# Attention over 64 heads: first and last pair head by head, loads in a new order, a fixed plan for the values

## The chip, the cores and the metric

The kernel runs on one core of a Trainium2 chip. The metric is the device time of one execution in microseconds (us). The profiler's span, from the first to the last instruction, is about 1.8 us shorter (134.32 us and 132.5 us for the profiled run of the kernel before). A run is called slow here when it is more than 1.5% above the fastest run of the same kernel; kernels are compared by their fast runs, and a difference under 2% is not called faster or slower. Five engines matter: TensorE (PE in the profile, with its weight loads as PEld), VectorE (DVE), ScalarE (ACT), GpSimd (POOL), and SyncE (SP), which issues most transfers.

## The reference

```python
q, k, v: float32 [8, 8, 512, 64]          # batch, heads, sequence, dim
scores = einsum('bhqd,bhkd->bhqk', q, k) / 8
attn   = exp(scores - max) ; attn = attn / attn.sum(-1)
out    = einsum('bhqk,bhkd->bhqd', attn, v)
```

The kernel leaves out the maximum and divides at the end: v carries a column of ones, so the value matmuls give the row sums as column 65.

## The kernel before

The 64 heads are 32 pairs. Both heads of a pair lie in one 128-row tile, 64 rows each. Scores are made transposed, in blocks of 128 keys x 512 queries. Two blocks form a group: one `st` buffer in PSUM, the memory that TensorE writes to (two banks; a bank is the unit in which the kernel shares it out), one exponential on ScalarE. A pair is four groups, numbered through from 0. The code is abridged:

```python
ps_st = tile_pool(bufs=3)   # scores, 2 banks each: 6 banks
ps_o  = tile_pool(bufs=1)   # o, the values' result: 1 bank
ps_t  = tile_pool(bufs=1)   # transposes: 1 bank
...
def values(g, h, part):                 # one part = four matmuls
    if part == 0:
        os[(g, h)] = ps_o.tile([P, NI, D + 1], FP32, tag="o")   # waits for the last reader
    for x in range(NI):
        nc.tensor.matmul(o[:, qc, :], blocks[...], vps[...])     # qc, c from part and x
    if part == NI - 1:
        normalise(g, h)                 # VectorE: reciprocal, product, o is free after it
...
fill = []                               # work that is put between the scores, in this order
for g in range(NP):
    for h in range(2):
        transposes(g + 2, 1 - h)        # two halves
        values(g, h, 0..3)
...
for m in range(steps):                  # after the scores of group m: up to 6 entries of fill,
    scores(m)                           # as far as their exponentials are LAG groups old
    ...
```

(A quota and the age of the exponentials decide how many entries follow. What comes of it in the steady state is: scores, all four value parts of head 0, four transposes, scores, all four parts of head 1, four transposes, scores, scores.) For the last pair both heads' values are summed key block by key block.

The softmax here doesn't subtract the row's maximum and nothing guards it: scores larger than these inputs give would overflow.

## Time and profile before

| | before |
|---|---|
| device time, median of the first 3 runs | 134.61 us (134.34 to 134.69) |
| span of the profiled run | 132.5 us |
| ScalarE busy | 119.3 us, 90% |
| TensorE busy, as recorded | 102.2 us, 77% |
| one pair (four groups) in the steady state | 3.67 us |
| first exponential | 6.04 us |
| scores of group 126 (of 128) to the end of the span | 132.5 - 122.93 = 9.6 us |

ScalarE is full in the middle, so the pair's 3.67 us is its time for four exponentials. The prediction below shows the lines.

Two kinds of lines are shown. A group line gives line of the kernel, engine, operation, output<-input, sizes and count, then busy us and mean ns of one, then the engine's idle time before them and what ended it. A timeline line starts with start and length in us; a bracket at its end gives the idle time before it and what ended that. `vp` is v, `pt` the exponentials, `tqk` the transposed q and k, `tp` a transpose's result, `ob` the divided output.

### The profile page before, as it was taken

How to read it: one execution, taken by the hardware profiler on the slowest of the kernel's cores; microseconds unless marked ns; L12 is line 12 of the kernel's file. 1: busy time of each engine (PE TensorE's matmuls, PEld its weight loads, DVE VectorE, ACT ScalarE, POOL GpSimd, SP SyncE). 2: the span in 40 equal slices, each digit the busy share in tenths (PEclk: the TensorE clock that was granted, in tenths of full speed). 3: DMA queues.
4: the chain of work that ended last, by engine and by line, in shares of the span. 5: the costliest groups of instructions: out<-in, count | busy, mean ns of one | idle time of the engine just before them, and what ended most of it. 6: DMA issues, size and time to landing. Idle time of an engine off the chain costs nothing.

```text
span 132.5 us, 3980 instructions
## 1 busy us (share of the span) xinstructions
PE 102.2 (77%) x1542; PEld 63.7 (48%) x1542; DVE 61.3 (46%) x196; ACT 119.3 (90%) x130; POOL 56.7 (43%) x107
## 2 busy tenths in 40 slices
PE   6737988777877778877788777898777877778650
PEld 2222755554555455555455544555544554454440
DVE  0412464455445555445544455544454445554231
ACT  3264999999999999999999999999999999999910
POOL 2268887544445555534444555534544445000000
PEclk9965799999999999999999999999999999999975
DMA  3999999989998999969999889949999990222231
GB/s 112 274 354 354 348 355 335 340 297 267 299 303 209 324 314 318 294 181 311 333 302 307 285 284 291 307 143 304 350 337 283 293 297 28 75 77 79 79 117 47
DMA packets 35123, 33.82 MB, mean 255 GB/s; under 512 B 2080, under 2 KB 35104, under 8 KB 35104
## 3 DMA queue, kind: packets, MB, share of 16 engines
q1 hardware_dynamic: 34832, 33.43, 79.0%
q8 instruction: 12, 0.20, 0.6%
q10 hardware_dynamic: 272, 0.13, 0.3%
q14 instruction: 7, 0.06, 0.2%
HBM read 25.17 MB, written 8.39 MB: 253 GB/s over the span
## 4 chain that ended last, share of the span: by engine, by line
ACT 41%; PE 33%; issue 13%; DVE 4%; DMA 4%; SPq 1%; POOL 0%; ACTq 0%
ACT pt L125 41%; PE o L157 16%; PE st L117 11%; PE tp L104 6%; DMA k<-in_k_dram 4%; DVE ob L136 3%; DVE rc L135 1%; DVE tqk L106 1%; POOL qkp L90 0%; SPq L176 0%; SPq L175 0%; SPq L174 0%; ACTq L125 0%
## 5 line engine op out<-in xcount | busy, mean ns | idle before, releaser
L125 ACT ACTIVATE pt<-st 128x1024 f16<-128x1024 f32 x128 | 117.7, 1351 | 4.7 <-PE st L117 4.7
L117 PE MATMUL st<-tqk 64*128 64x512 f16 x256 | 45.0, 389 | 14.2 <-ACT pt L125 14.0
L157 PE MATMUL o<-vp,pt 128*128 128x65 f16 x1024 | 44.6, 196 | 8.1 <-DVE ob L136 8.1
L157 PEld LDWEIGHTS <-pt 128*128 128x128 f16 x1024 | 36.6, 99 | 24.7 <-DVE ob L136 16.5
L90 POOL CAST qkp<-k 128x512 f16<-128x512 f32 x31 | 19.0, 613 | 46.9 <-PE tp L104 44.3
L135 DVE RECIPROCAL rc<-o 128x4 f32<-128x4 f32 x64 | 11.7, 183 | 57.3 <-PE o L157 57.3
L117 PEld LDWEIGHTS <-tqk 64*128 64x128 f16 x256 | 14.3, 94 | 32.7 <-issue 24.5
L136 DVE TENSOR_TENSOR ob<-o,rc 128x256 f32<-128x256 f32 x64 | 27.2, 425 | 2.5 <-DVE rc L135 0.3
L106 DVE COPY tqk<-tp 128x512 f16<-128x512 f16 x62 | 25.7, 415 | 4.6 <-PE tp L104 4.6
L104 PE MATMUL tp<-ident,qkp 128*128 128x128 f16 x248 | 24.7, 224 | 2.9 <-POOL qkp L90 1.9
L83 POOL CAST vp<-v 128x512 f16<-128x512 f32 x32 | 19.7, 616 | 3.6 <-DMA v<-in_v_dram 2.7
L90 POOL CAST qkp<-q 128x512 f16<-128x512 f32 x31 | 19.0, 613 | 0.6 <-DMA q<-in_q_dram 0.2
L104 PEld LDWEIGHTS <-qkp 128*128 128x128 f16 x248 | 15.4, 99 | 3.9 <-POOL qkp L90 3.6
L232 PE MATMUL warm<-zeros 128*128 128x512 f16 x6 | 2.7, 629 | 1.2 <-DVE zeros L226 1.2
L186 ACT ACT_TABLE_LOAD x1 | 1.3, 1283 | 1.2 <-PEq L272 1.2
L232 PEld LDWEIGHTS <-zeros 128*128 128x128 f16 x6 | 0.7, 136 | 2.3 <-DVE zeros L226 1.2
L184 DVE CAST qkp<-k 128x256 f16<-128x256 f32 x1 | 0.3, 294 | 2.9 <-DMA k<-in_k_dram 2.9
L187 POOL CAST qkp<-k 128x256 f16<-128x256 f32 x1 | 0.4, 396 | 2.9 <-DMA k<-in_k_dram 2.9
L186 ACT CAST qkp<-q 128x256 f16<-128x256 f32 x1 | 0.4, 405 | 1.3 <-DMA q<-in_q_dram 1.3
L193 PEld LDWEIGHTS <-qkp 128*128 128x128 f16 x2 | 0.1, 106 | 1.4 <-DVE qkp L184 1.4
L193 PE MATMUL tp<-ident,qkp 128*128 128x128 f16 x2 | 0.3, 229 | 0.5 <-DVE qkp L184 0.5
L226 DVE MEMSET zeros<- 128x256 uint32 x1 | 0.3, 272 | 0.9 <-PEq L272 0.9
(15 smaller groups left out, 3.6 us busy)
## 6 DMA issues: line engine op xcount, KB each, us to landing
q<-in_q_dram SPq DMA_DIRECT2D x32, 256.0 KB, 4.3
v<-in_v_dram SPq DMA_DIRECT2D x32, 256.0 KB, 4.6
k<-in_k_dram SPq DMA_DIRECT2D x31, 256.0 KB, 4.2
out_dram<-ob SPq DMA_DIRECT2D x31, 256.0 KB, 3.2
out_dram<-ob SPq DMA_DIRECT2D x2, 128.0 KB, 2.2
k<-in_k_dram ACTq DMA_DIRECT2D x1, 128.0 KB, 3.3
k<-in_k_dram SPq DMA_DIRECT2D x1, 128.0 KB, 3.1
```

The costliest lines, as they stand in the source:

```text
L83: nc.gpsimd.tensor_copy(out=vps[g % NV][:, :, :, 0:D], in_=raw[g]["v"][:, :, :, :])
L90: nc.gpsimd.tensor_copy(out=t[:, n].rearrange("p i (h d) -> p h i d", h=2), in_=raw[g][name][:, :, :, :],)
L104: nc.tensor.transpose(tp[:, i, :], qkp[g][:, n, i, :], ident)
L106: nc.vector.tensor_copy(out=tqk[g][:, n, :], in_=tp.rearrange("p i c -> p (i c)"))
L117: nc.tensor.matmul(st[:, x, :], tqk[g][po : po + 64, 1, c * P : (c + 1) * P], tqk[g][po : po + 64, 0, :], start=True, stop=True,)
L125: nc.scalar.activation(out=pt[:, 0:size, :], in_=st[:, 0:size, :], func=EXP, scale=scale)
L135: nc.vector.reciprocal(out=rc[:, :, :], in_=o[:, :, D : D + 1])
L136: nc.vector.tensor_tensor(out=ob[:, h], in0=o[:, :, 0:D], in1=rc[:, :, :].broadcast_to([P, NI, D]), op=AluOp.mult,)
L157: nc.tensor.matmul(o[:, qc, :], blocks[NB * g + 2 * c + h][:, qc * P : (qc + 1) * P], vps[g % NV][:, h, c, :], start=(c == 0 and (qc == 0 ...
L186: nc.scalar.copy(q16[:, 1], tiles["q"][:, 1])
L187: nc.gpsimd.tensor_copy(out=k16[:, :, 2:4], in_=tiles["k"][:, :, 2:4])
L232: nc.tensor.matmul(warm[:, 0, :], zeros[:, 0:P], zeros[:, :], start=True, stop=True)
```

## The change

The intent is to shorten both ends. The first pair's q and k are loaded as halves, one head each, and its scores are taken head by head. Each later pair's q and k are loaded before the v of the pair before it. The last pair is taken head by head too, with the last group split into two of one block, so that little is left after the last exponential. The quota rule is replaced by a fixed list.

```diff
-    NB = 2 * NI
-    TOTAL = NP * NB
+    stream = []
+    for g in range(NP):
+        if g in (0, LAST):
+            stream += [(g, c, h) for h in range(2) for c in range(NI)]
+        else:
+            stream += [(g, c, h) for c in range(NI) for h in range(2)]
+    groups = [stream[n : n + 2] for n in range(0, len(stream), 2)]
+    tail = groups.pop()
+    groups += [[b] for b in tail]
 ...
     def values(g, h, part):
+        last = g == LAST and h == 1
         if part == 0:
-            os[(g, h)] = ps_o.tile([P, NI, D + 1], FP32, tag="o", name=f"o_{g}_{h}")
+            pool, tag = (ps_t, "tp") if last else (ps_o, "o")
+            os[(g, h)] = pool.tile([P, NI, D + 1], FP32, tag=tag, name=f"o_{g}_{h}")
 ...
+    def first_loads():
+        for h in range(2):
+            nc.scalar.dma_start(out=tk[:, h], in_=source(k, 0)[:, h])
+            nc.sync.dma_start(out=tq[:, h], in_=source(q, 0)[:, h])
 ...
-    for g in range(NP):
-        for h in range(2):
-            if g + 2 < NP:
-                for part in range(2):
-                    fill.append((-1, transposes, (g + 2, 1 - h, part)))
-            for part in range(NI):
-                need = ...
-                fill.append((need, values, (g, h, part)))
+    for g in range(NP - 1):
+        if g == 0:
+            fill[2] += [(transposes, (1, 1)), (transposes, (1, 0))]
+        else:
+            fill[4 * g + 1].append((transposes, (g + 1, 1)))
+            fill[4 * g + 2].append((transposes, (g + 1, 0)))
+        todo = [(values, (g, h, part)) for h in range(2) for part in range(NI)]
+        for m, n in ((6, 2), (7, 3), (8, 2), (9, 1)) if g < LAST - 1 else ((6, 3), (7, 3), (8, 2)):
+            fill[4 * g + m] += todo[:n]
+            todo = todo[n:]
+    fill[M - 1] += [(values, (LAST, h, part)) for h in range(2) for part in range(NI)]
 ...
+        load(1, "kq")
+        load(0, "v")
+        for g in range(2, 6):
+            load(g, "kq")
+            load(g - 1, "v")
```

Cut: the first pair's casts and transposes, now per head, the loop that walks the list, and the transposes, which are now made one pair ahead instead of two.

More of the change, by code (lines that the diff above doesn't have):

```diff
@@ L13 @@
 AluOp = mybir.AluOpType
-GROUP = 2
-ST_BUFS = 3
-LAG = 3
 @with_exitstack
@@ L36 @@
     ppb = H // 2
-    NB = 2 * NI
-    TOTAL = NP * NB
+    LAST = NP - 1
+    stream = []
[7 more added lines that the diff above has]
+    groups += [[b] for b in tail]
+    M = len(groups)
     cpool = ctx.enter_context(tc.tile_pool(name="const", bufs=1))
@@ L43 @@
     tpool = ctx.enter_context(tc.tile_pool(name="tqk", bufs=4))
-    ppool = ctx.enter_context(tc.tile_pool(name="pt", bufs=24 // GROUP))
+    ppool = ctx.enter_context(tc.tile_pool(name="pt", bufs=12))
     opool = ctx.enter_context(tc.tile_pool(name="out", bufs=4))
-    ps_st = ctx.enter_context(
-        tc.tile_pool(name="ps_st", bufs=ST_BUFS, space=bass.MemoryType.PSUM)
-    )
+    ps_st = ctx.enter_context(tc.tile_pool(name="ps_st", bufs=3, space=bass.MemoryType.PSUM))
     ps_o = ctx.enter_context(tc.tile_pool(name="ps_o", bufs=1, space=bass.MemoryType.PSUM))
@@ L63, with load_tile, load, cast_qk @@
     obs = {}
-    def where(g):
-        return g // ppb, 2 * (g % ppb)
     def source(src, g):
-        b, h = where(g)
+        b, h = g // ppb, 2 * (g % ppb)
         return src[b, h : h + 2].rearrange("h (p i) d -> p h i d", i=NI)
-    def load(g):
+    def load_tile(g, name):
+        t = lpool.tile([P, 2, NI, D], FP32, tag=f"{name}32", name=f"{name}32_{g}")
+        raw.setdefault(g, {})[name] = t
+        return t
+    def load(g, names):
         if g >= NP:
             return
-        tiles = {}
-        for name, src in (("k", k), ("q", q), ("v", v)):
-            t = lpool.tile([P, 2, NI, D], FP32, tag=f"{name}32", name=f"{name}32_{g}")
+        for name in names:
+            src = {"q": q, "k": k, "v": v}[name]
+            t = load_tile(g, name)
             nc.sync.dma_start(out=t[:, :, :, :], in_=source(src, g))
-            tiles[name] = t
-        raw[g] = tiles
     def cast_v(g):
         nc.gpsimd.tensor_copy(out=vps[g % NV][:, :, :, 0:D], in_=raw[g]["v"][:, :, :, :])
-    def cast(g):
+    def cast_qk(g):
         if g >= NP:
@@ L94, in cast, with transposes @@
         qkp[g] = t
-        cast_v(g)
-    def transposes(g, n, part):
-        if part == 0:
-            if n == 1:
-                tqk[g] = tpool.tile([P, 2, S], FP16, tag="tqk", name=f"tqk_{g}")
-            tps[g] = ps_t.tile([P, NI, P], FP16, tag="tp", name=f"tp_{g}_{n}")
-        tp = tps[g]
-        for i in (2 * part, 2 * part + 1):
+    def transposes(g, n):
+        if g >= NP:
+            return
+        if n == 1:
+            tqk[g] = tpool.tile([P, 2, S], FP16, tag="tqk", name=f"tqk_{g}")
+        tp = ps_t.tile([P, NI, P], FP16, tag="tp", name=f"tp_{g}_{n}")
+        for i in range(NI):
             nc.tensor.transpose(tp[:, i, :], qkp[g][:, n, i, :], ident)
-        if part == 1:
-            nc.vector.tensor_copy(out=tqk[g][:, n, :], in_=tp.rearrange("p i c -> p (i c)"))
+        nc.vector.tensor_copy(out=tqk[g][:, n, :], in_=tp.rearrange("p i c -> p (i c)"))
     def scores(m):
-        n0 = m * GROUP
-        size = min(GROUP, TOTAL - n0)
-        st = ps_st.tile([P, GROUP, S], FP32, tag="st", name=f"st_{m}")
-        pt = ppool.tile([P, GROUP, S], FP16, tag="pt", name=f"pt_{m}")
-        for x in range(size):
-            g, j = divmod(n0 + x, NB)
-            c, h = divmod(j, 2)
+        grp = groups[m]
+        size = len(grp)
+        st = ps_st.tile([P, 2, S], FP32, tag="st", name=f"st_{m}")
+        pt = ppool.tile([P, 2, S], FP16, tag="pt", name=f"pt_{m}")
+        for x, (g, c, h) in enumerate(grp):
             po = 64 * h
@@ L123, in scores @@
             )
-            blocks[n0 + x] = pt[:, x, :]
+            blocks[(g, c, h)] = pt[:, x, :]
         nc.scalar.activation(
@@ L141, in normalise @@
         )
-        last = g == NP - 1
-        if last:
+        if g == LAST:
             nc.sync.dma_start(out=source(out, g)[:, h], in_=ob[:, h])
@@ L148, in values @@
     def values(g, h, part):
+        last = g == LAST and h == 1
         if part == 0:
-            os[(g, h)] = ps_o.tile([P, NI, D + 1], FP32, tag="o", name=f"o_{g}_{h}")
+            pool, tag = (ps_t, "tp") if last else (ps_o, "o")
+            os[(g, h)] = pool.tile([P, NI, D + 1], FP32, tag=tag, name=f"o_{g}_{h}")
         o = os[(g, h)]
-        last = g == NP - 1
         for x in range(NI):
@@ L158, in values @@
                 o[:, qc, :],
-                blocks[NB * g + 2 * c + h][:, qc * P : (qc + 1) * P],
+                blocks[(g, c, h)][:, qc * P : (qc + 1) * P],
                 vps[g % NV][:, h, c, :],
@@ L166, in values @@
             normalise(g, h)
-    def first_pair():
-        tiles = {}
-        for name in ("k", "q", "v"):
-            tiles[name] = lpool.tile([P, 2, NI, D], FP32, tag=f"{name}32", name=f"{name}32_0")
-        raw[0] = tiles
-        nc.scalar.dma_start(out=tiles["k"][:, :, 0:2], in_=source(k, 0)[:, :, 0:2])
-        nc.sync.dma_start(out=tiles["q"][:, :, :, :], in_=source(q, 0))
-        nc.sync.dma_start(out=tiles["k"][:, :, 2:4], in_=source(k, 0)[:, :, 2:4])
-        nc.sync.dma_start(out=tiles["v"][:, :, :, :], in_=source(v, 0))
@@ L178, in first_transposes @@
-    def first_transposes():
-        tiles = raw[0]
-        t = qpool.tile([P, 2, NI, P], FP16, tag="qkp", name="qkp_0")
-        qkp[0] = t
-        k16 = t[:, 1].rearrange("p i (h d) -> p h i d", h=2)
-        q16 = t[:, 0].rearrange("p i (h d) -> p h i d", h=2)
-        nc.vector.tensor_copy(out=k16[:, :, 0:2], in_=tiles["k"][:, :, 0:2])
-        nc.vector.tensor_copy(out=q16[:, 0], in_=tiles["q"][:, 0])
-        nc.scalar.copy(q16[:, 1], tiles["q"][:, 1])
-        nc.gpsimd.tensor_copy(out=k16[:, :, 2:4], in_=tiles["k"][:, :, 2:4])
-        cast_v(0)
-        tqk[0] = tpool.tile([P, 2, S], FP16, tag="tqk", name="tqk_0")
-        tk = ps_t.tile([P, NI, P], FP16, tag="tp", name="tp_0_1")
-        tq = ps_o.tile([P, NI, P], FP16, tag="o", name="tp_0_0")
-        for i in range(2):
-            nc.tensor.transpose(tk[:, i, :], t[:, 1, i, :], ident)
-        nc.vector.tensor_copy(
-            out=tqk[0][:, 1, 0:256], in_=tk[:, 0:2].rearrange("p i c -> p (i c)")
-        )
-        for i in range(NI):
-            nc.tensor.transpose(tq[:, i, :], t[:, 0, i, :], ident)
-        nc.vector.tensor_copy(out=tqk[0][:, 0, :], in_=tq.rearrange("p i c -> p (i c)"))
-        tk2 = ps_t.tile([P, 2, P], FP16, tag="tp", name="tp_0_2")
-        for i in range(2):
-            nc.tensor.transpose(tk2[:, i, :], t[:, 1, 2 + i, :], ident)
-        nc.vector.tensor_copy(
-            out=tqk[0][:, 1, 256:512], in_=tk2.rearrange("p i c -> p (i c)")
-        )
@@ L208 @@
-    fill = []
-    for n in (1, 0):
-        for part in range(2):
-            fill.append((-1, transposes, (1, n, part)))
-    for g in range(NP):
-        for h in range(2):
-            if g + 2 < NP:
-                for part in range(2):
-                    fill.append((-1, transposes, (g + 2, 1 - h, part)))
-            for part in range(NI):
-                need = NB * g + 2 * (part if g == NP - 1 else NI - 1) + h
-                fill.append((need, values, (g, h, part)))
-    AHEAD = 5
@@ L222 @@
-    with tc.manual_schedule():
-        first_pair()
-        for g in range(1, AHEAD):
-            load(g)
+    def first_loads():
+        tk = load_tile(0, "k")
+        tq = load_tile(0, "q")
+        for h in range(2):
+            nc.scalar.dma_start(out=tk[:, h], in_=source(k, 0)[:, h])
+            nc.sync.dma_start(out=tq[:, h], in_=source(q, 0)[:, h])
+    def first_transposes():
+        tk, tq = raw[0]["k"], raw[0]["q"]
+        tqk[0] = tpool.tile([P, 2, S], FP16, tag="tqk", name="tqk_0")
+        halves = []
+        for h in range(2):
+            t = cpool.tile([P, 2, NI, P], FP16, name=f"qkp_0_{h}")
+            nc.gpsimd.memset(t[:, :, :, 64 * (1 - h) : 64 * (1 - h) + 64], 0.0)
+            halves.append(t)
+        for h in range(2):
+            t, s = halves[h], slice(64 * h, 64 * h + 64)
+            if h == 0:
+                nc.vector.tensor_copy(out=t[:, 1, 0:2, s], in_=tk[:, h, 0:2])
+                nc.vector.tensor_copy(out=t[:, 0, 0:2, s], in_=tq[:, h, 0:2])
+                nc.scalar.copy(t[:, 0, 2:4, s], tq[:, h, 2:4])
+                nc.gpsimd.tensor_copy(out=t[:, 1, 2:4, s], in_=tk[:, h, 2:4])
+            else:
+                nc.gpsimd.tensor_copy(out=t[:, 1, :, s], in_=tk[:, h])
+                nc.gpsimd.tensor_copy(out=t[:, 0, :, s], in_=tq[:, h])
+        for h in range(2):
+            t, s = halves[h], slice(64 * h, 64 * h + 64)
+            pk = ps_t.tile([P, NI, P], FP16, tag="tp", name=f"tp_0_1_{h}")
+            pq = ps_o.tile([P, NI, P], FP16, tag="o", name=f"tp_0_0_{h}")
+            for n, i in ((1, 0), (1, 1), (0, 0), (0, 1), (0, 2), (0, 3), (1, 2), (1, 3)):
+                if (n, i) == (1, 2):
+                    pk2 = ps_st.tile([P, 2, P], FP16, tag="st", name=f"tp_0_2_{h}")
+                dst = pq[:, i, :] if n == 0 else pk[:, i, :] if i < 2 else pk2[:, i - 2, :]
+                nc.tensor.transpose(dst, t[:, n, i, :], ident)
+                if (n, i) == (1, 1):
+                    nc.vector.tensor_copy(
+                        out=tqk[0][s, 1, 0:256], in_=pk[s, 0:2].rearrange("p i c -> p (i c)")
+                    )
+                elif (n, i) == (0, 3):
+                    nc.vector.tensor_copy(
+                        out=tqk[0][s, 0, :], in_=pq[s].rearrange("p i c -> p (i c)")
+                    )
+                elif (n, i) == (1, 3):
+                    nc.vector.tensor_copy(
+                        out=tqk[0][s, 1, 256:512], in_=pk2[s].rearrange("p i c -> p (i c)")
+                    )
+            if h == 0:
+                scores(0)
+                scores(1)
@@ new lines @@
+    fill = [[] for _ in range(M)]
+    for g in range(NP - 1):
+        if g == 0:
+            fill[2] += [(transposes, (1, 1)), (transposes, (1, 0))]
+        else:
+            fill[4 * g + 1].append((transposes, (g + 1, 1)))
[4 more added lines that the diff above has]
+            todo = todo[n:]
@@ L226 @@
+    fill[M - 1] += [(values, (LAST, h, part)) for h in range(2) for part in range(NI)]
+    with tc.manual_schedule():
+        first_loads()
+        load(1, "kq")
[3 more added lines that the diff above has]
+            load(g - 1, "v")
         nc.vector.memset(zeros[:, :], 0.0)
@@ L229 @@
             nc.gpsimd.memset(vps[n][:, :, :, D : D + 1], 1.0)
-        warm = ps_st.tile([P, GROUP, S], FP32, tag="st", name="warm")
+        warm = ps_st.tile([P, 2, S], FP32, tag="st", name="warm")
         for n in range(6):
@@ L233 @@
         first_transposes()
-        cast(1)
-        cast(2)
-        done = 0
-        steps = (TOTAL + GROUP - 1) // GROUP
-        for m in range(steps):
-            n0 = m * GROUP
-            if n0 % NB < GROUP:
-                g = n0 // NB
-                load(g + AHEAD)
-                cast(g + 3)
-            scores(m)
-            quota = max(0.0, (n0 + GROUP) * len(fill) / TOTAL)
-            budget = GROUP * 3
-            while done < len(fill) and done < quota and budget > 0:
-                need, what, args = fill[done]
-                if need >= (m - LAG + 1) * GROUP:
-                    break
-                what(*args)
-                done += 1
-                budget -= 1
-        while done < len(fill):
-            need, what, args = fill[done]
-            what(*args)
-            done += 1
+        cast_qk(1)
+        cast_v(0)
+        cast_qk(2)
+        cast_v(1)
+        for m in range(M):
+            g, x = divmod(m, 4)
+            if x == 0:
+                load(g + 6, "kq")
+                if g + 5 < NP:
+                    load(g + 5, "v")
+                cast_qk(g + 3)
+                if g + 2 < NP:
+                    cast_v(g + 2)
+            if m >= 2:
+                scores(m)
+            for what, args in fill[m]:
+                what(*args)
 _INS = ['q', 'k', 'v']
```

## The prediction

> **What bounds the kernel now.** I read the page's busy row and its slices first, because they say which engine is full and where it is not.
>
> ```profile
> PE 102.2 (77%) x1542; PEld 63.7 (48%) x1542; DVE 61.3 (46%) x196; ACT 119.3 (90%) x130; POOL 56.7 (43%) x107
> ...
> ACT  3264999999999999999999999999999999999910
> ```
>
> ScalarE (ACT) is full in all slices but the first four and the last two. Its groups, and the TensorE (PE) groups that feed it, are these; the next view is ScalarE's own part of the timeline.
>
> ```profile
> L125 ACT ACTIVATE pt<-st 128x1024 f16<-128x1024 f32 x128 | 117.7, 1351 | 4.7 <-PE st L117 4.7
> L117 PE MATMUL st<-tqk 64*128 64x512 f16 x256 | 45.0, 389 | 14.2 <-ACT pt L125 14.0
> ```
>
> ```profile
> 6.04 2.86 ACT L125 ACTIVATE pt<-st 128x1024 f16<-128x1024 f32 x3 [1.81 <-PE st L117]
> 11.75 114.80 ACT L125 ACTIVATE pt<-st 128x1024 f16<-128x1024 f32 x125 [2.85 <-PE st L117]
> ```
>
> One exponential has a latency of 1.351 us but they overlap: 125 in 114.80 us is (114.80 - 1.351)/124 = 0.915 us from start to start, or 3.66 us for a pair of heads (four groups). So the run is: 6.04 us until the first exponential, a hole of 2.85 us after three, 125 without a hole, and 132.5 - 126.55 = 5.95 us after the last. TensorE waits for ScalarE, which is the sign of its slack. How much slack, and of what kind, is in one period of the steady state, from the timeline:
>
> ```profile
> 71.59 0.39 PE L117 MATMUL st<-tqk 64*128 64x512 f16 x2 [0.48 <-ACT pt L125]
> ...
> 71.92 0.56 PEld L157 LDWEIGHTS <-pt 128*128 128x128 f16 x16 [0.23 <-issue]
> ...
> 72.41 0.24 PEld L104 LDWEIGHTS <-qkp 128*128 128x128 f16 x4
> ...
> 72.64 0.18 DVE L135 RECIPROCAL rc<-o 128x4 f32<-128x4 f32 x1 [1.27 <-PE o L157]
> 72.75 0.10 PEld L117 LDWEIGHTS <-tqk 64*128 64x128 f16 x2
> ...
> 72.85 0.42 DVE L136 TENSOR_TENSOR ob<-o,rc 128x256 f32<-128x256 f32 x1
> ...
> 73.33 0.56 PEld L157 LDWEIGHTS <-pt 128*128 128x128 f16 x16 [0.49 <-DVE ob L136]
> ```
>
> I name the pieces S (a pair of score matmuls), V (four value matmuls, one of the four parts of a head) and T (four transposes). From start to start: S followed by V 0.33 us; four V 0.49, so one V 0.12; T followed by S 0.35. The order is S, 4V, T, S, wait, 4V, T, S, S. The wait is the point: there is one buffer for the output o, so the second head's first V may start only when VectorE has divided the first head's o. From the last V's slot (72.41) to the next V (73.33) is 0.92 us: matmul latency 0.2, reciprocal 0.2, product 0.42, handovers 0.1. In the kernel before, T and S (0.68 us) fill nearly all of it. Near the end, where no T is left, it stands bare:
>
> ```profile
> 123.25 0.56 PEld L157 LDWEIGHTS <-pt 128*128 128x128 f16 x16 [0.23 <-issue]
> ...
> 124.67 0.31 PEld L157 LDWEIGHTS <-pt 128*128 128x128 f16 x8 [0.86 <-DVE ob L136]
> 125.03 0.10 PEld L117 LDWEIGHTS <-tqk 64*128 64x128 f16 x2
> ```
>
> 124.67 - 123.25 = 1.42 us, less 0.49 for the four V, is 0.93 us of standing still. The same lines show that two V followed by S take 0.36, where 0.245 would be their share: a step from V to S costs about 0.11 more.
>
> **What the Trainium skill says.** "TensorE: Matmul & The Clock Gate", Part 2, "Step-by-step: what each phase is for": only weight loads are pulled ahead, the matmuls stay in program order. The trace agrees: nothing overtakes the V that waits at 124.67. So whatever follows a waiting V in the program waits with it. "TensorEngine Tiling (Array Packing)", "Key Properties": changing the tiling mode drains TensorE. Scores use 64 rows, values and transposes 128; the 0.11 us at each change from V to S fits this, though nothing isolates the cause. "DMA: Bandwidth & Descriptors", "Anatomy of one DMA", gives a constant cost of about 2.0 us per transfer; here 128 KB to the output land in 2.2 us (median), so the last transfer cannot shrink below that by being small.
>
> **The change, part by part.**
>
> *Head.* The first pair's q and k now arrive as 128 KB per head, so the first head waits for 256 KB instead of 512 KB. The old loads landed at 3.8 (q) and 4.0 to 4.4 (k). I put the first halves at 3.3 to 3.5 (2.2 us of latency after the issue at 0.74, plus sharing). The warm-up matmuls hold TensorE until about 3.8, so the first scores come at about 5.0 and the first exponential at about 5.4, 0.6 earlier. The hole at 8.9 came from the second pair's k, which was issued at 2.24 and landed at 7.61, 5.37 us in the chain of waits. Moved ahead of v it is issued at about 1.74, and should land where v did before (its cast started at 6.23). Its cast (0.61), q's cast (0.61, q landing near 7.5), two T with the copy between them (0.61, 0.42) put the fourth score group at about 9 and the seventh, S6, where the values begin, at about 11. Before, exponential 6 started at 11.75 + 3 x 0.915 = 14.5, its scores somewhat earlier. The head is worth 2 to 3 us.
>
> *Steady state.* The old rule put all of a head's V in one group. The fixed plan spreads them 2, 3, 2, 1, so that a pair is, in TensorE's program order: S, V00, V01, T, S, V02, V03, V10, S, V11, V12, S, V13, T, and again S, V00. V10 stands directly behind V03 and needs o divided: 0.93 us with nothing to fill it, in every pair. V00 of the next pair stands behind V13, T, S: of 0.93 us, T and S fill 0.68. Work it out as a loop, from V02:
>
> V02 V03 0.245, bare wait 0.93, V10 and the step to S 0.235, S 0.33, V11 V12 and the step 0.36, S 0.33, V13 0.12, wait 0.93 (T and S inside it), V00 V01 0.245, T 0.35, S 0.33. Sum 4.4 us.
>
> The same by content: four S 1.3, eight V 1.0, two T 0.7, two extra steps 0.2: 3.2 us of work, below ScalarE's 3.66. With 0.93 bare and 0.25 half-filled, 4.4. So TensorE's order becomes the bound, with ScalarE idle 0.7 us in each pair. Without any cost for the mode steps, S at 0.21, it would still be near 3.85. I take 4.3. It applies from S6 to S126, 30 periods: 129 us, where ScalarE alone would need 30 x 3.66 = 110. The loss is 19 us.
>
> *Tail.* Head-by-head order and one-block groups were to leave only one V after the last exponential, instead of two heads (126.55 to 129.73). But the plan's pieces of pair 30 come late. From S126: S with both blocks on the same rows 0.54, rest of a wait 0.4, three V 0.37, S and step 0.43, V 0.12, bare wait 0.93, two V and step 0.36, S 0.32, two V 0.25, bare wait 0.93, eight V 0.98, then matmul latency, two divisions in a row, about 1.0: 6.6 us. The last transfer to the end of the span takes as before 132.5 - 129.73 = 2.8. Together 9.4. ScalarE is done well before and saves nothing here.
>
> Sum: 11 + 129 + 9.4 = 149.4 us of span. The median time is 134.61 for a span of 132.5, so 2.1 more: about 151.5; I name 151, since prefetched weight loads may trim a little.
>
> **The rivals.**
>
> *ScalarE stays the bound.* Three score buffers let TensorE run up to two groups ahead, and ScalarE was 90% busy. If the waits were absorbed, the time would be 134.6 less 2 to 3 (head) less 1.5 to 2 (tail), about 130.5. For it: the plan looks balanced, and TensorE stood idle at each ACT wait (0.48 us as recorded, more if the ends of matmuls were real). Against it: buffers absorb an uneven spacing, not a period that is too long, and the period contains two dependent chains through VectorE that sum above 3.66 whatever ScalarE does.
>
> *TensorE bound, but milder.* If S costs 0.21 and the mode steps nothing, the loop is 3.85, and the time 151.5 - 30 x 0.45 = 138. The isolated S, V steps of 0.33 in the trace speak against it.
>
> *Transfers become the bound.* Inputs and outputs are 33.4 MB; early slices reach 354 GB/s, so 34 MB need about 95 us. Not near.
>
> *Slower clock.* The clock row falls to 0.57 in the tail of before, where TensorE is idle for long. If gaps of 0.93 us also lowered it in the steady state, T, V and S would stretch and the time could pass 157. The gaps are short beside the working stretches, so I give it little.
>
> **Range and chances.** The period is the uncertain term: 4.05 to 4.5 gives 30 x 0.45 = 13.5 us of width, from about 144 to 157.5; the head adds 1 us either way, and the mild rival pulls the lower end. I take 142 to 157. For a time below 137.3 the period would have to be under 3.83, which needs both waits nearly hidden: 0.09 in all, of it 0.05 for faster than 131.9, for the case that I misread which tile V10 waits for.
>
> **What would show it.** Right: ScalarE idle before score matmuls some 30 times or more, about 20 us in all; values waiting for the division (PE o <- DVE ob), 8.1 us in 32 waits before, rising to about 30 us in some 60 waits of about 0.9 and 0.25 us; a period of 4.3 us; first exponential near 5.4 and no hole over 1.5 us before the fifth. Wrong: a ScalarE row with 9 in every middle slice, a period of 3.66, or the V after V03 starting within 0.3 us.

## The result, and the profile after

The first four executions of the changed kernel took 154.38, 159.99, 155.65 and 157.87 us, median 156.76, against 134.48 (133.95 to 134.69) before. A ratio is the mean time of one kernel's fast runs over that of the other's of the same rounds, so not quite the ratio of the medians; here it is 1.153 (1.143 to 1.164). The two longer executions count as slow and are left out of it. Four more executions gave 154.0 to 155.5 us and 1.152. They were run at other times.

The page of the changed kernel, its busy row, ScalarE's slices and the groups that answer to those shown of before:

```profile
PE 116.9 (77%) x1550; PEld 68.2 (45%) x1550; DVE 64.9 (43%) x199; ACT 122.5 (80%) x131; POOL 58.2 (38%) x111
...
ACT  4589988988888898888888988888898888889810
...
L126 ACT ACTIVATE pt<-st 128x1024 f16<-128x1024 f32 x129 | 120.9, 1024 | 22.2 <-PE st L118 22.2
L158 PE MATMUL o<-vp,pt 128*128 128x65 f16 x1024 | 60.1, 197 | 29.5 <-DVE ob L137 29.5
```

No engine is full any more. ScalarE stands idle 22.2 us waiting for scores. The recorded mean length of an exponential fell from 1351 to 1024 ns, but the instruction isn't faster: four of them in 3.77 us, as below, are still 0.92 us from start to start. (That it no longer queues behind its neighbour is my reading.) Who waits for whom, in the view of waits (total us, times, longest), first before, then after:

```profile
PE o L157 <- DVE ob L136: 8.1, 32, 0.8
```

```profile
PE o L158 <- DVE ob L137: 29.5, 62, 0.8
ACT pt L126 <- PE st L118: 22.2, 32, 2.0
```

Two waits of TensorE per pair instead of one, and one hole of ScalarE per pair. ScalarE's timeline after (start, length, what; the last line is one of some thirty alike):

```profile
5.65 3.02 ACT L126 ACTIVATE pt<-st 128x1024 f16<-128x1024 f32 x3 [2.02 <-PE st L118]
9.41 8.36 ACT L126 ACTIVATE pt<-st 128x1024 f16<-128x1024 f32 x9 [0.74 <-PE st L118]
...
70.92 3.77 ACT L126 ACTIVATE pt<-st 128x1024 f16<-128x1024 f32 x4 [0.64 <-PE st L118]
```

The first hole has shrunk from 2.85 to 0.74 us, which was intended. Then four exponentials and a hole of 0.64 us, again and again. Here is what TensorE and VectorE do in one such period:

```profile
72.47 0.30 PEld L158 LDWEIGHTS <-pt 128*128 128x128 f16 x8 [0.49 <-DVE ob L137]
...
73.44 0.31 PEld L158 LDWEIGHTS <-pt 128*128 128x128 f16 x8 [0.23 <-issue]
...
73.91 0.18 DVE L136 RECIPROCAL rc<-o 128x4 f32<-128x4 f32 x1 [0.26 <-PE o L158]
74.13 0.42 DVE L137 TENSOR_TENSOR ob<-o,rc 128x256 f32<-128x256 f32 x1
...
74.60 0.18 PEld L158 LDWEIGHTS <-pt 128*128 128x128 f16 x4 [0.86 <-DVE ob L137]
...
74.84 0.10 PEld L118 LDWEIGHTS <-tqk 64*128 64x128 f16 x2
...
75.16 0.31 PEld L158 LDWEIGHTS <-pt 128*128 128x128 f16 x8 [0.23 <-issue]
...
76.88 0.31 PEld L158 LDWEIGHTS <-pt 128*128 128x128 f16 x8 [0.48 <-DVE ob L137]
77.12 0.30 PEld L108 LDWEIGHTS <-qkp 128*128 128x128 f16 x4
```

At 72.47 come head 0's first two parts, at 73.44 its last two, at 73.91 the division starts, and only at 74.60 may head 1's first part enter the single o buffer. Nothing stands between in the program, so TensorE does nothing for 0.9 us. The scores behind it (74.84) come late, and ScalarE has its hole. At 76.88 the next pair's first part waits for head 1's division, behind scores and transposes that hide most of it. One period before and after. The numbers are its length, then the busy time of TensorE, its weight loads, VectorE, ScalarE and GpSimd (with counts), the granted TensorE clock as a share of full speed, the share of the DMA engines, and GB/s:

```profile
71.59:75.26 3.67, 3.00 (x48) 1.92 (x48) 1.88 (x6) 3.67 (x5) 1.73 (x3) 1.00 0.94 300
```

```profile
72.47:76.88 4.41, 3.48 (x48) 2.07 (x48) 1.97 (x7) 3.77 (x5) 1.74 (x3) 1.00 0.59 188
```

The same 48 matmuls at the same full clock, 4.41 us instead of 3.67. That splits the difference of the two spans, 152.6 - 132.5 = 20.1 us:

| stretch | before | after | difference |
|---|---|---|---|
| start to scores of group 6 | 12.82 | 10.49 | -2.3 |
| group 6 to group 126, 30 pairs | 110.1 (3.67 each) | 132.1 (4.40 each) | +22.0 |
| group 126 to the end | 9.6 | 10.0 | +0.4 |

In these two profiles the head gained, the tail didn't, and the middle lost 22 us. (How much of the head's gain is the change, and how much the run, comes up in experiment 8.)

### The profile page after: what moved, and what is told of

Read it like the earlier page. It is cut to its first block, busy times and chain, and to the rows that moved or that the text cites. A ratio compares the mean times of both kernels' runs of the same rounds, so it can differ in the third digit from the quotient of the medians.

```text
span 152.6 us, 4004 instructions
## 1 busy us (share of the span) xinstructions
PE 116.9 (77%) x1550; PEld 68.2 (45%) x1550; DVE 64.9 (43%) x199; ACT 122.5 (80%) x131; POOL 58.2 (38%) x111
## 4 chain that ended last, share of the span: by engine, by line
PE 62%; DVE 26%; issue 4%; DMA 3%; SPq 1%; ACT 1%; POOL 0%
PE o L158 36%; PE st L118 20%; DVE ob L137 18%; DVE rc L136 8%; PE tp L108 6%; DMA k<-in_k_dram 3%; SPq L85 1%; ACT pt L126 1%; SPq L174 1%; POOL qkp L95 0%
## 5 line engine op out<-in xcount | busy, mean ns | idle before, releaser
L126 ACT ACTIVATE pt<-st 128x1024 f16<-128x1024 f32 x129 | 120.9, 1024 | 22.2 <-PE st L118 22.2
L158 PE MATMUL o<-vp,pt 128*128 128x65 f16 x1024 | 60.1, 197 | 29.5 <-DVE ob L137 29.5
L158 PEld LDWEIGHTS <-pt 128*128 128x128 f16 x1024 | 41.1, 99 | 63.8 <-DVE ob L137 40.7
L118 PE MATMUL st<-tqk 64*128 64x512 f16 x256 | 51.4, 386 | 1.0 <-DVE tqk L208 0.8
L118 PEld LDWEIGHTS <-tqk 64*128 64x128 f16 x256 | 12.6, 92 | 11.8 <-issue 0.9
L108 PEld LDWEIGHTS <-qkp 128*128 128x128 f16 x248 | 16.6, 97 | 1.5 <-issue 1.1
L202 PEld LDWEIGHTS <-qkp 128*128 128x128 f16 x16 | 1.0, 104 | 1.3 <-issue 1.3
L204 DVE COPY tqk<-tp 64x256 f16<-64x256 f16 x2 | 0.6, 288 | 1.5 <-PE tp L202 1.5
L182 POOL MEMSET qkp<- 128x512 f16 x2 | 1.0, 528 | 0.0
L208 DVE COPY tqk<-tp 64x512 f16<-64x512 f16 x2 | 0.8, 422 | 0.0
```

The source lines that it names most:

```text
L108: nc.tensor.transpose(tp[:, i, :], qkp[g][:, n, i, :], ident)
L118: nc.tensor.matmul(st[:, x, :], tqk[g][po : po + 64, 1, c * P : (c + 1) * P], tqk[g][po : po + 64, 0, :], start=True, stop=True,)
L126: nc.scalar.activation(out=pt[:, 0:size, :], in_=st[:, 0:size, :], func=EXP, scale=scale)
L158: nc.tensor.matmul(o[:, qc, :], blocks[(g, c, h)][:, qc * P : (qc + 1) * P], vps[g % NV][:, h, c, :], start=(c == 0 and (qc == 0 or not la ...
L202: nc.tensor.transpose(dst, t[:, n, i, :], ident)
```

## The experiments

My theory: the place of the value parts around the one o buffer makes the whole loss. Rivals: the other parts of the change (loads, transposes one pair ahead, pairs head by head); TensorE's changes between 64-row scores and 128-row values, now more of them; a lack of score buffers; the clock. All runs gave correct results. "Changed kernel" means its fast runs, 155.0 us in the mean, unless another is named.

### 1. Whole heads together again

```diff
-        for m, n in ((6, 2), (7, 3), (8, 2), (9, 1)) if g < LAST - 1 else ((6, 3), (7, 3), (8, 2)):
+        for m, n in ((6, 4), (7, 4)):
```

> The changed kernel with one thing undone: all four value parts of a head stand together again, heads in two successive groups, so that transposes and scores stand between the first head's last part and the second head's first. Theory (the order around the single o buffer costs the time): the period returns to 3.66 us, ScalarE has no hole after the fourth exponential, and what remains is the head's and the tail's gain: 130 to 131.5 us, against 134.5 before. Rival (the loads, the transposes only one pair ahead, or the head-by-head pairs cost the time): it stays above 145 us.

Measured: 133.67, 132.53, 133.83, 130.64 us, the two upper ones slow; ratio of the fast runs to before 0.982 (0.972 to 0.992), so no clear gain over before. But the plan alone makes the loss: with all other parts of the change kept, some 23 us are gone. The profile fell on a slow run. The first line is of this run's ScalarE, the second of its TensorE, the third of the changed kernel's TensorE:

```profile
17.16 110.17 ACT L126 ACTIVATE pt<-st 128x1024 f16<-128x1024 f32 x121 [0.29 <-PE st L118]
```

```profile
5.14 1.86 PE L118 MATMUL st<-tqk 64*128 64x512 f16 x4 [0.29 <-DVE tqk L208]
```

```profile
5.03 1.02 PE L118 MATMUL st<-tqk 64*128 64x512 f16 x4 [0.40 <-DVE tqk L208]
```

From 17.16 us on there is no hole. But the first four score matmuls took 1.86 us instead of 1.02, and the fourth exponential starts at 11.95 instead of 9.41 us: TensorE ran at about half speed there. The granted clock reads 1.00 in this stretch all the same; in experiment 9's profile, a fast run, six score matmuls take 1.88 us as they do here (at 10.88), and there the clock reads 0.50. The Trainium skill ("TensorE: Matmul & The Clock Gate", Part 1, "What's actually happening") says that the clock is released by activity in a window of about 3.4 us that runs freely, so the warm-up differs from run to run. That fits the clusters of times, and experiment 3 shows such windows; why this run was slow, one profile doesn't prove.

### 2. One value part moved by one place

```diff
-((6, 2), (7, 3), (8, 2), (9, 1))
+((6, 2), (7, 2), (8, 3), (9, 1))
```

> The changed kernel with one value part moved by one place: the plan is 2, 2, 3, 1 in place of 2, 3, 2, 1, so the second head's first part stands behind the next scores instead of before them. Theory (bare wait for o): the scores now lie inside the 0.93 us wait; by the loop of the prediction with the durations of the changed kernel's trace the period falls from 4.41 to about 3.96 us, the time by 30 x 0.45 = 13.5 us, to about 142. Rival (TensorE pays for its changes between 64-row scores and 128-row values, each pair of scores standing alone): the number of changes is the same, so 4.41 us and about 155 us stay.

Measured: median 142.86 us (141.6 in the two fast runs, 144.1 and 144.7 in the slow ones). The period in the trace, from one wait for o to the next of its kind (70.74 to 74.72), is 3.98 us:

```profile
70.74 0.43 PE L158 MATMUL o<-vp,pt 128*128 128x65 f16 x8 [0.19 <-DVE ob L137]
...
74.72 0.43 PE L158 MATMUL o<-vp,pt 128*128 128x65 f16 x8 [0.19 <-DVE ob L137]
```

The number of changes between scores and values is as it was, so those changes don't make this part of the loss (for the rest of it see experiment 6). Moving four matmuls behind two saves 13 us, as the loop says.

### 3 and 4. The division done twice, in both kernels

```diff
-        nc.vector.tensor_tensor(out=ob[:, h], ...)
+        for _ in range(2):
+            nc.vector.tensor_tensor(out=ob[:, h], ...)
```

In the changed kernel:

> The changed kernel with each division by the row sums done twice on VectorE (same result). Theory: both waits for o in a period grow by 0.34 to 0.42 us, and nothing hides it: period 5.1 to 5.25 us, time 175 to 181 us. Rival (o is not what TensorE waits for): VectorE goes from 43% to about 60% busy, still far from full, and the time stays near 155 us.

In the kernel before:

> The kernel before with the same doubled division. Theory: TensorE's own order needs about 3.0 us per pair there, with 0.42 more 3.4, still under ScalarE's 3.66: the period does not change, only the last three divisions, which lie on the final chain, add about 1.0 to 1.3 us: 135.5 to 136 us. Rival (a doubled division costs the same in any order): about 20 us more, 155 us.

Both expectations were wrong in size. The changed kernel took 193.0 and 210.0 us. Its period is 5.33 us where the clock is full, so 0.92 us longer: 0.46 us for each of the two waits, one whole product with its handover. That is 28 us of the 38 to 55 us. The two waits of one period:

```profile
82.30 0.30 PE L159 MATMUL o<-vp,pt 128*128 128x65 f16 x4 [1.19 <-DVE ob L138]
...
85.03 0.43 PE L159 MATMUL o<-vp,pt 128*128 128x65 f16 x8 [0.65 <-DVE ob L138]
```

Part of the rest is the clock. Its row on the page (tenths of full speed in 40 slices), and two periods, the first with a slow window in it (granted clock 0.72 in the mean, against 1.00):

```profile
PEclk9859789969999979999789999699999699998555
```

```profile
38.88:44.98 6.10, 4.68 (x54) 2.62 (x52) 2.82 (x8) 4.09 (x5) 1.74 (x3) 0.72 0.54 182
44.98:50.30 5.32, 3.48 (x54) 2.06 (x50) 2.82 (x8) 3.88 (x5) 1.74 (x3) 1.00 0.48 143
```

Read in finer windows, the granted clock falls to 0.50 six times between 21.8 and 151.6 us, for 3.41 us each time (38.87 to 42.28, for one), and costs the period 0.8 us. The starts lie 17.1 or 27.3 us apart, five or eight times 3.41, which agrees with the freely running window quoted in experiment 1. The changed kernel's two profiles, with waits of 0.74 and 0.19 us, show no such stretch before 147.5 us. That the longer waits bring it on is the likely reading; no run changed the clock alone. Of the 38.6 us by which the profiled span grew, 27.6 are the waits, some 5 these stretches, 1.8 the head, and the remaining 4 to 5 the last pair and the end, at half clock from 175.4 us on. The run of 210 us has no profile.

The kernel before rose to 140.3 us (140.0 and 140.5; ratio 1.047), not to 135.5 to 136. Its value parts in the steady state:

```profile
71.71 0.56 PEld L158 LDWEIGHTS <-pt 128*128 128x128 f16 x16 [0.94 <-DVE ob L137]
...
73.58 0.56 PEld L158 LDWEIGHTS <-pt 128*128 128x128 f16 x16 [0.38 <-DVE ob L137]
...
75.46 0.56 PEld L158 LDWEIGHTS <-pt 128*128 128x128 f16 x16 [0.94 <-DVE ob L137]
```

I had asked whether TensorE's work, with the longer waits, fits under 3.66 us. The right question is how long the o buffer is held. Here a head holds it for 1.87 us (0.49 of matmuls and 1.38 until it is free), two heads for 3.75: more than ScalarE's 3.67, and so the period. That explains 30 x 0.08 = 2.4 us; the divisions at the end 1.3 or more. Taken by stretches the trace has 3.7 us more from group 6 to 126, 3.0 more after it (the end ran at half clock from 128.2 us), and 0.9 less in the head; I didn't take it further apart.

Seen this way the undoubled kernels are plain too. In the kernel before a head holds o for 0.49 + 0.93 = 1.42 us, a pair for 2.84 of 3.67, with 0.8 to spare. In the changed kernel scores and transposes stand *between* a head's parts, so o is held through them: 74.60 - 72.47 = 2.13 us for head 0 and 76.88 - 74.60 = 2.28 for head 1. Their sum is the 4.41 us of the period. (It has to be: the next part starts 0.05 us after the division, so no time is left over between two heads. In the kernel before 0.8 us is left.)

### 5 and 6. The same plan with two o buffers

The three pools take eight banks (3 x 2, 1 and 1), and I did not go beyond that. So one score buffer (two banks) is given up for the second o, and the control gives it up with one o buffer all the same.

```diff
-    ps_st = tile_pool(name="ps_st", bufs=3)        # both runs: bufs=2
-    ps_o  = tile_pool(name="ps_o",  bufs=1)        # second run only: bufs=2
```

> Control for the next run: the changed kernel, its fill plan kept, with two score buffers instead of three. One score group fewer lies ready, the waits for o are as they were. Theory (o is held all the time): period 4.45 to 4.7 us, 155 to 163 us. Rival (three score buffers are what the plan needs): much worse, over 170 us.

> The changed kernel, its fill plan kept to the letter, with two score buffers and, in the room of the third, a second buffer for o. No value part waits for a division any more. Theory (the single o buffer, held while other work stands between a head's parts, sets the period): TensorE's work of 3.2 to 3.3 us fits under ScalarE's 3.66, with some loss from having only two score buffers: period 3.7 to 3.95 us, 132 to 140 us, and the waits for the division vanish. Rival (the spread order itself, by its changes of mode, is too long for TensorE): no faster than the control, over 150 us.

Measured: the control 158.8 and 159.9 us, ratio 1.188, its period 4.41 us, as in the changed kernel (the value part after the bare wait comes at 73.78 and at 78.19). What it adds to the changed kernel isn't in the period, which I had put a little longer, but in the head: the group whose exponential starts at 18.10 us in the changed kernel's second profile starts at 21.62 here. The second run, with the fill plan kept to the letter, took 132.1 and 134.1 us, ratio 0.992. Its group of value matmuls on the page:

```profile
L158 PE MATMUL o<-vp,pt 128*128 128x65 f16 x1024 | 54.5, 196 | 0.0
```

No idle time is left before them, where the changed kernel had 29.5 us, and the period is 3.67 us (72.88 to 76.55):

```profile
72.88 0.30 PE L158 MATMUL o<-vp,pt 128*128 128x65 f16 x4
...
76.55 0.30 PE L158 MATMUL o<-vp,pt 128*128 128x65 f16 x4
```

The buffer was the cause, not the spread of the parts as such: the same order with a second buffer is as fast as ScalarE, even with one score buffer fewer.

### 7. The old last pair

Experiment 1 with the last pair as before: heads interleaved, a last group of two blocks, both heads' values in key order in the single o buffer.

```diff
-        if g in (0, LAST):
+        if g == 0:
-    tail = groups.pop()
-    groups += [[b] for b in tail]
-        last = g == LAST and h == 1
+        last = g == LAST
-            pool, tag = (ps_t, "tp") if last else (ps_o, "o")
+            pool, tag = (ps_o, "o")
```

> Whole heads together as in the first experiment, and the last pair undone as well: heads interleaved, a last group of two blocks, both heads' values in key order in the single o buffer. Theory: from the scores of group 126 to the end of the span as in the kernel before, about 9.6 us, against about 8.2 with the new last pair; the time is 1.0 to 1.6 us above that of the first experiment. Rival (the tail does nothing, the output transfer sets it): no difference.

Measured: 131.21, 131.26, 131.23 us, and one slow run of 134.38; ratio 0.978 (0.975 to 0.982, no clear gain). From the scores of group 126 to the end of the span it is 129.4 - 120.53 = 8.9 us; in experiment 1, a slow run, it is 131.9 - 123.66 = 8.2 us, and as much in the fast run of experiment 8 (128.8 - 120.58), which has the same last pair. The new last pair gains 0.6 us, less than I expected, and the times, blurred by the first microseconds, don't show it. The 9.6 us of the kernel before held something else: its last 16 value matmuls took 1.08 us (at 128.00) at a granted clock of 0.50, here 0.67 at full clock.

### 8. v before the next pair's q and k

```diff
-        load(1, "kq"); load(0, "v"); then load(g, "kq"), load(g - 1, "v")
+        load(0, "v"); then load(g, "kqv") for each pair
```

> Whole heads together as in the first experiment, half loads kept, but each pair's v loaded before the next pair's q and k as in the kernel before. Theory: with the half loads the second pair's k is cast 1.3 us before TensorE reaches its transposes (6.2 against 7.5 us in the changed kernel's trace), so one 256 KB transfer ahead of it (0.75 us each) is nearly hidden: 0 to 0.8 us above the first experiment. Rival (moving q and k ahead of v makes the head's gain): 1.4 us or more above it.

Measured: 130.8, 132.4, 131.1, 130.5 us, ratio 0.979 (0.972 to 0.985, no clear gain), and the fourth exponential at 9.51 us (9.41 in the changed kernel). The old order of loads costs nothing that can be seen. The second pair's k is cast at 6.59 us then, and TensorE comes to its transposes at 7.64. So the head's gain doesn't come from moving q and k ahead of v, but from the rest of the new head. What of that rest does it (the halves, or TensorE's clock in that stretch, which read 0.66 from 6 to 12 us in the profile of before and 1.00 in the changed kernel's) I did not separate. And the head differs from run to run: over all profiles with the new head and three score buffers the fourth exponential starts between 9.41 and 11.95 us (without the extra matmuls of experiment 10), with the old head at 11.75 (before) and 10.86 (experiment 4). So the 2.3 us of the table above are the difference of two profiles, not a sure gain of the change.

### 9. A version to beat both

Experiment 1, and in the last two pairs the second head's o goes to the transposes' bank, which is free by then, so that no value part in the tail waits.

```diff
+        other = g >= LAST - 1 and h == 1
-            pool, tag = (ps_t, "tp") if last else (ps_o, "o")
+            pool, tag = (ps_t, "tp") if other else (ps_o, "o")
```

> Meant to beat both: whole heads together, new loads and new last pair, and the second head of the last two pairs put into the bank that the transposes no longer need, so that no value part in the tail waits for a division. Theory: 0.9 us less than the first experiment in the tail, about 2.4 us less than before there: 129.5 to 131 us where the first microseconds run at full clock, 1 to 2 more where they don't. Rival: ScalarE's last exponential sets the end, and it is as the first experiment.

Measured: 129.74, 129.98, 129.99, 131.50 us fast, and 132.43, 132.97, 133.28 slow; ratio of the fast runs 0.968 (0.964 to 0.973). Group 126 to the end is 129.7 - 122.15 = 7.6 us, 0.7 less than in experiment 1. It beats the kernel before, slow runs included, but its seven runs lie in clusters. The profile fell on the 131.50 us: its granted clock is 0.50 from 8.8 to 15.6 us, and 0.968 in the mean over the run, where the three runs near 129.9 have 0.996 to 0.998. The slow runs have 0.993 to 0.997 and no profile; their reason stays open.

### 10. A busier head

The kernel of experiment 9 with two matmuls on zeros, overwritten by the scores that follow, ahead of the first and of the third score group.

```diff
+        for n in range({0: 2, 2: 2}.get(m, 0)):
+            nc.tensor.matmul(st[:, 0, :], zeros[:, 0:P], zeros[:, :], start=True, stop=True)
```

> The two-bank version with two idle score-shaped matmuls on zeros (their results overwritten by the scores) ahead of the first and the third score group, where TensorE waits for VectorE's copies. Theory: runs differ by whether the clock is granted in the first 17 us, and a busier TensorE gets it more often: the runs near 133 us vanish, median 130 to 131. Rival (the phase of the clock's window decides, whatever is done): the same two clusters, median as before or up to 0.5 us later.

Measured: 130.78, 130.68, 131.08, 130.39, 130.36 us, all fast, ratio 0.974 (0.971 to 0.977). The fourth exponential starts at 10.35 us, so the extra matmuls cost 0.9 us against the best case, and no run near 133 was seen. Over all runs its mean is 130.7 us, that of experiment 9 131.4, though the fast runs of experiment 9 are the faster ones (ratio 0.968). The mean clock is 0.996 to 1.000 in all five. They make it likely, not certain, that the upper clusters are gone: experiment 9 ran on another chip, and beside these five, without the extra matmuls, ran experiment 8, where only one run of four exceeds 131.1 us.

### 11. The changed kernel once more

> The changed kernel once more, unchanged, to see its spread of 154 to 160 us beside the others. Theory: its period is all TensorE and VectorE at full clock, so runs differ by windows at half clock, in the head and by single windows of 3.4 us in the middle (0.8 us each, as with the doubled division): times again from 154 to 160, a profile of a longer run shows such windows, and the period outside them is 4.41 us. Rival: the period itself differs from run to run.

Measured: 154.32, 155.52, 154.01, 154.51 us, ratio 1.152 (1.147 to 1.157), period 4.41 us again, and no half-speed window in the middle of the profiled run. Runs of 158 and 160 us did not come, so what lengthened those two stays open. No profile fell on such a run, and the mean clock does not settle it (0.974 in the run of 160.0 us, 0.967 in the fast one of 155.65).

## Why the prediction was right

- **The period.** Predicted: TensorE's order, tied to VectorE through o, takes 4.4 us by the sum of its pieces; 4.3 was taken. Measured: 4.41, with the pieces as they were added up: from 73.44 to 74.60 the two parts and the bare wait take 1.16 us (predicted 1.18); only the transposes with their step to the scores take 0.41 instead of 0.35 (72.71 to 73.12). Experiments 1, 2 and 6 show that it is this loop: it goes with the order (3.67), shrinks by the amount of one moved part (3.98), and goes with a second buffer although the order stays (3.67).
- **The waits.** Predicted about 30 us in some 60 waits, ScalarE idle about 20 us in 30 or more. Measured 29.5 in 62, and 22.2 in 32.
- **The head.** Predicted group 6 at 11 and the first exponential at 5.4 us. Measured 10.49 and 5.65. But the reason given for the end of the 2.85 us hole, q and k ahead of v, fell with experiment 8.
- **The tail.** Predicted 9.4 us from group 126, with nothing gained. Measured 10.0, against 9.6 before.
- **The sum.** Predicted 149.4 us of span, 151 us of time. The profiled span is 152.6: the head was 0.5 us shorter than predicted, the middle 3.1 longer, the end 0.6. The 3 us are the 0.1 us per pair by which I went below my own sum of 4.4; the text gives no reason for it but the milder case, and the cost of the changes of mode was there in full. The 2.1 us from span to time mixed two runs (1.8 within one). The median of the first call, 156.8, lies just under the range's upper end because that call holds two slow runs; that it stayed inside is luck, the period isn't. The fast runs are at 154.4 and 155.7, and the later median is 154.4.
- **The rivals.** "ScalarE stays the bound" is what experiment 1 shows once the order is undone, near the 130.5 us named there (its fast runs took 130.6 and 132.5). The milder case, with no cost for changes of mode, was refuted by the trace: a pair of scores between values takes 0.32 us in the changed kernel too (74.84 to 75.16; and by the prediction's own terms that case is 3.82 us, not 3.85). The slower clock is no part of the period in the changed kernel's two profiled runs, but in experiment 3, with waits half a microsecond longer, half-speed stretches do appear.
- **What I would word otherwise.** The prediction counts what fills each wait. Experiment 4 shows that the count to make first is how long the buffer is held: from the trace of before that is 2 x (1.42 + 0.42) = 3.68 us with a second product, already at ScalarE's 3.67 (measured 3.75), where counting TensorE's work gave 3.4.

## What to carry to other kernels

For each buffer of which there is only one, add up from the trace how long it is held per period, from its first writer to its last reader's end, with the work that the new order puts between them: if the sum exceeds the busiest engine's time, expect that sum as the period, whatever the engines' busy shares say. Spreading a producer's parts evenly between other work lengthens the holding; keep the parts together, and put the other work into the wait between the last part and the release. When ends of a kernel are tuned, check the middle first: 30 periods times 0.7 us outweigh any head.

## What the Trainium skill lacked or had wrong

- "TensorE: Matmul & The Clock Gate" warns of idle gaps beyond about 3 us, and of micro-idles in one kernel without their size. Here six half-speed windows of 3.41 us (0.8 us lost in each) came with waits of 1.19 and 0.65 us in a period of 5.33 us, and none in the middle with waits of 0.74 and 0.19 us in 4.41 us.
- The same page gives the warm-up as under 1% of a typical kernel. Here a half-speed stretch of 6.8 us in the head goes with 131.50 us, against 129.7 to 130.0 us for the same kernel's other fast runs, so over 1% (experiment 9; ScalarE, which has no slack afterwards, starts later). And the clock row can read 9 where four score matmuls take 1.86 instead of 1.02 us (experiment 1).
- "TensorEngine Tiling (Array Packing)" says that a change of tiling mode drains TensorE, with no figure. In these traces two value parts take 0.245 us before other 128-row work and 0.36 before 64-row scores, so about 0.11 us more; that the drain is the cause was not isolated.
- "DMA: Bandwidth & Descriptors" gives about 2.0 us of constant cost, fitted on transfers that GpSimd issues; I found no such fit for those that SyncE issues. The last two 128 KB stores, from SyncE, landed in 2.2 us before and 1.7 us after (medians), so what is constant in them is below 1.7 us here.
- "Perfetto Trace Analysis" says that a gap which repeats can mean too few buffers; I found no page that adds up the time for which a buffer is held, as a bound of its own. Here it set the period in four kernels (4.41, 3.98, 3.75 and 5.33 us).
